# Moving a convolution branch under attention, and a reciprocal root from ScalarE and VectorE to GpSimd, in a conformer layer on eight cores

## The chip, the cores and the metric

The kernel runs on all 8 cores of one Trainium2 chip (two dies, cores 0 to 3 and 4 to 7). Each core computes 2048 of the 2 x 8192 tokens and needs nothing from the others. The metric is the device time of the slowest core, in microseconds (us). Some executions are slow: the cores of one or both dies show a lower granted clock; such runs are left out of every comparison. PE is the tensor engine, ACT is ScalarE, DVE is VectorE, POOL is GpSimd.

## The reference

```python
u = rms_norm(x, norm_mix_pre)
a_val, a_gate, q, k, v = split(u @ w_in)              # 512 + 512 + 3 * 512 columns
h = a_val * sigmoid(a_gate)                           # GLU
h = causal_depthwise_conv(h, dw_w, dw_b)              # 31 taps
conv_out = silu(layer_norm(h, ln_g, ln_b))            # norm over the 512 channels
attn_out = chunked_band_attention(q, k, v, rel_bias)  # 8 heads, chunks of 64, 8 chunks back
mixed = concat([conv_out, attn_out]) @ w_out
h = x + rms_norm(mixed, norm_mix_post)
u = rms_norm(h, norm_ffn_pre)
f = (gelu(gate) * val of causal_depthwise_conv(u @ w_up)) @ w_down
out = h + rms_norm(f, norm_ffn_post)
```

## The kernel before

Every operation is recorded with the buffers that it reads and writes. A list scheduler with a cost model then fixes the order of each engine's instructions when the kernel is built. In the traces each engine takes its queue in that order, and this matters for most of what follows (in wup_early below two DMA issues at the head of POOL's queue stood 3.68 us, and the small operation behind them began 0.08 us after they were done).

The stages, in order, are: input projections; four attention slots, one for each group of 512 tokens (numbered 2 to 5), with other work of PE woven in as fill; the convolution of chunk 0 and of chunk 1 (1024 tokens each); its layer norm, Silu and an exchange through DRAM, which turns the split layout of the convolution into the time layout of the projection; the output projection in 17 tiles of up to 128 tokens; and the FFN. The FFN uses the same banks of PSUM as the projection, so it begins when the projection is nearly done. In the profile's lines `ps` is a tile in PSUM, which PE's matmuls write here, and `big` is one in SBUF, where their operands are (as in `PE L905 MATMUL ps<-big`). Here, in short form, are a chunk's tail and the projection's reciprocal root (rstd):

```python
def conv_norm(ch):                                    # before
    for g in range(0, 32, 4):
        dve.tensor_tensor(v, v, mean, subtract)       # 4 groups of channels x 129, fp32
        dve.tensor_tensor(v, v, rstd, mult)
        for i in range(4):
            act.activation(cs[g + i], cf[g + i], Silu, scale, bias)
    sp.dma_start(out=cd, in_=cs)                      # the exchange: write ...
    sp.dma_start(out=raw, in_=cd)                     # ... and read back in the other layout
    for c in range(4):                                # rearrange (q s) to (s q)
        (act.copy if c == 3 else dve.tensor_copy)(coT[c], raw[c])
...
def wo_sq(i, src):                                    # two for each tile of the projection
    act.activation(junk, src, Square, accum_out=ssq)
    act.activation(tmp, ssq, Sqrt, scale=1.0 / D, bias=eps)
    dve.reciprocal(rstd, tmp)
...
for t in range(17 + 5):                               # the projection, a software pipeline
    for lag, f in ((5, wo_tp), (4, wo_u), (3, wo_sq2), (2, wo_res), (1, wo_sq1), (0, wo_mm)):
        if 0 <= t - lag < 17:
            f(t - lag)
```

`wo_mm` fills one of three pairs of PSUM banks. `wo_sq1` squares it, `wo_res` scales it (DVE) and adds x (DVE). `wo_sq2` squares the sum, `wo_u` scales that (DVE), and `wo_tp` transposes it for the FFN (PE, then an ACT copy).

The softmax here doesn't subtract the row's maximum and nothing guards it: scores larger than these inputs give would overflow.

Of the kernel before, what the change touches and what calls it, by code (L numbers as in the profile page):

```python
# [9 lines left out]
BF16 = mybir.dt.bfloat16  # L10
# [8 lines left out]
AHEAD = {2: 0, 3: 0, 4: 0, 5: 600}  # L19
# [293 lines left out]
def build_program():  # L313
# [11 lines left out]
    cvp_d = dr("cvp", [128, 3 * 32])  # L325
# [11 lines left out]
    CP = {0: 130, 1: 128}  # L337
    cd = {c: nc.dram_tensor("cd%d" % c, [8, 128, 4 * CP[c]], BF16).ap() for c in CN}

    with ExitStack() as es:  # L340
# [38 lines left out]
        blkf = const("blkf", [128])  # L379
# [3 lines left out]
        cvp = const("cvp", [3, 32])  # L383
# [3 lines left out]
        epsc = const("epsc", [1])  # L387
# [30 lines left out]
        cwt = sb("cwt", 151504, [32, 5, 128], BF16)  # L418

        g2b = sb("g2b", gfp.lo, [1024])  # L420
        cfb = [sb("cf0", 102352, [32, 129]), sb("cf1", 12800, [32, 128])]
        st4 = [sb("lnst%d" % i, 118864 + i * 516, [129]) for i in range(4)]
        cs = [sb("cs0", 120960, [32, 130], BF16), sb("cs1", 29184, [32, 128], BF16)]
        cbq = sb("cbq", 200912, [32, 129], BF16)
        raw = [sb("raw0", 120960, [8, 4, 130], BF16), sb("raw1", 120960, [8, 4, 128], BF16)]
        coT = [sb("coT0", 102352, [4, 1032], BF16), sb("coT1", 102352 + 8256, [4, 1024], BF16)]
        Wo = sb("Wo", 135120, [8, 1024], BF16)
# [48 lines left out]
        S.op("pool", lambda: pool.memset(epsc.ap, EPS), writes=[epsc])  # L476
# [301 lines left out]
        def weave(steps, fill):  # L778
            total = sum(c for c, _ in fill)
            done, k = 0.0, 0  # L780
            for i, s_ in enumerate(steps):
                s_()
                while k < len(fill) and done + fill[k][0] / 2 <= total * (i + 1) / len(steps):
                    fill[k][1]()
                    done += fill[k][0]
                    k += 1
            while k < len(fill):
                fill[k][1]()
                k += 1

        c_lo = {0: 0, 1: 129}

        def conv_units(ch):
            N, cf = CN[ch], cfb[ch]
            units = []
            g = 0
            while g < 32:
                ng = min(3, 32 - g)

                def f(g=g, ng=ng):  # L800
                    b = nbank()
                    for i in range(ng):
                        for d in range(5):
                            o_ = c_lo[ch] + 4 - d
                            S.mm(lambda i=i, d=d, o_=o_: pe.matmul(  # L805
                                b.ap[:, i * N:(i + 1) * N], lhsT=cwt.ap[:, g + i, d, :], rhs=hP.ap[:, g + i, o_:o_ + N],
                                start=(i == 0 and d == 0), stop=(i == ng - 1 and d == 4), skip_group_check=True),
                                reads=[cwt[(g + i) // 8], hP[0], hP[1]] + [hP[q] for q in ((2, 3) if ch == 0 else (3, 4, 5))],
                                writes=[b], last=(i == ng - 1 and d == 4), n=145)
                    v = lambda: b.ap[:, :ng * N].rearrange("p (g s) -> p g s", g=ng)  # L810
                    S.op("dve", lambda: dve.scalar_tensor_tensor(
                        out=cf.ap[:, g:g + ng, :N], in0=v(), scalar=0.5,
                        in1=cvp.ap[:, 0, g:g + ng].unsqueeze(2).to_broadcast([128, ng, N]), op0=ALU.mult, op1=ALU.add),
                        reads=[b, cvp], writes=[cf[g + i] for i in range(ng)], n=ng * N)
                    S.bias += 400 * ch
                    S.op("act", lambda: act.activation(out=cbq.ap[:, g:g + ng, :N], in_=cf.ap[:, g:g + ng, :N], func=AF.Square),
                         reads=[cf[g + i] for i in range(ng)], writes=[cbq[g + i] for i in range(ng)], n=ng * N)
                    S.bias -= 400 * ch
                units.append((0.08 * 5 * ng, f))
                g += ng  # L820
            return units

        def conv_stats(ch):
            N, cf = CN[ch], cfb[ch]
            mean, var, t2, rs = st4
            b = nbank()
            for g in range(32):
                S.mm(lambda g=g: pe.matmul(b.ap[:, 0:N], lhsT=blkf.ap, rhs=cf.ap[:, g, :N], start=(g == 0), stop=False, skip_group_check=True),
                     reads=[blkf, cf[g]], writes=[b], last=(g % 8 == 7), n=4 * N)
            for g in range(32):  # L830
                S.mm(lambda g=g: pe.matmul(b.ap[:, N:2 * N], lhsT=blk.ap, rhs=cbq.ap[:, g, :N], start=False, stop=(g == 31), skip_group_check=True),
                     reads=[blk, cbq[g]], writes=[b], last=(g == 31), n=N)
            S.op("dve", lambda: dve.tensor_scalar(out=mean.ap[:, :N], in0=b.ap[:, 0:N], scalar1=1.0 / 512, scalar2=None, op0=ALU.mult),
                 reads=[b], writes=[mean], n=N)
            S.op("dve", lambda: dve.tensor_tensor(out=t2.ap[:, :N], in0=mean.ap[:, :N], in1=mean.ap[:, :N], op=ALU.mult),
                 reads=[mean], writes=[t2], n=N)
            S.op("dve", lambda: dve.scalar_tensor_tensor(out=var.ap[:, :N], in0=b.ap[:, N:2 * N], scalar=1.0 / 512, in1=t2.ap[:, :N],
                                                         op0=ALU.mult, op1=ALU.subtract),
                 reads=[b, t2], writes=[var], n=N)
            S.op("dve", lambda: dve.tensor_scalar(out=var.ap[:, :N], in0=var.ap[:, :N], scalar1=0.0, scalar2=EPS, op0=ALU.max, op1=ALU.add),  # L840
                 reads=[var], writes=[var], n=N)
            S.op("dve", lambda: dve.reciprocal(out=t2.ap[:, :N], in_=var.ap[:, :N]), reads=[var], writes=[t2], n=N, f=8.0)
            S.op("act", lambda: act.activation(out=rs.ap[:, :N], in_=t2.ap[:, :N], func=AF.Sqrt), reads=[t2, DH["exps"]], writes=[rs], n=N + 3000)

        def conv_norm(ch):
            N, cf = CN[ch], cfb[ch]
            mean, var, t2, rs = st4
            for g in range(0, 32, 4):
                keys = [cf[g + i] for i in range(4)]
                v = cf.ap[:, g:g + 4, :N]  # L850
                S.op("dve", lambda: dve.tensor_tensor(out=v, in0=v, in1=mean.ap[:, :N].unsqueeze(1).to_broadcast([128, 4, N]), op=ALU.subtract),
                     reads=keys + [mean], writes=keys, n=4 * N)
                S.op("dve", lambda: dve.tensor_tensor(out=v, in0=v, in1=rs.ap[:, :N].unsqueeze(1).to_broadcast([128, 4, N]), op=ALU.mult),
                     reads=keys + [rs], writes=keys, n=4 * N)
                for i in range(4):
                    S.op("act", lambda i=i: act.activation(out=cs[ch].ap[:, g + i, :N], in_=cf.ap[:, g + i, :N], func=AF.Silu,  # L856
                                                           scale=cvp.ap[:, 1, g + i:g + i + 1], bias=cvp.ap[:, 2, g + i:g + i + 1]),
                         reads=[cf[g + i], cvp], writes=[cs[ch][g + i]], n=N)
            S.dma("sp", "cw%d" % ch, lambda: sp.dma_start(
                out=cd[ch].rearrange("q (c a) z -> (q c) (a z)", c=16), in_=cs[ch].ap.rearrange("p g s -> p (g s)")),  # L860
                reads=[cs[ch][g] for g in range(32)], writes=[DH["cd%d" % ch]], kb=1024)
            S.dma("sp", "cr%d" % ch, lambda: sp.dma_start(
                out=raw[ch].ap.rearrange("p q c s -> p q (c s)"), in_=cd[ch].rearrange("q p z -> p q z")),
                reads=[DH["cd%d" % ch]], writes=[raw[ch]], kb=1024)
            for c in range(4):
                o_ = coT[ch].ap[:, c, :].rearrange("p (s q) -> p s q", q=8)
                i_ = raw[ch].ap[:, :, c, :CN[ch]].rearrange("p q s -> p s q")
                if c == 3:
                    S.op("act", lambda o_=o_, i_=i_: act.copy(out=o_, in_=i_), reads=[raw[ch]], writes=[coT[ch][c]], n=2200)
                else:  # L870
                    S.op("dve", lambda o_=o_, i_=i_: dve.tensor_copy(out=o_, in_=i_), reads=[raw[ch]], writes=[coT[ch][c]], n=1030)
# [271 lines left out]
        def slot(g):  # L1143
            if g == 2:
                pre = pa_units(1) + pa_units(2)
            else:
                pre = pa_units(g)
# [121 lines left out]
```

## Time and profile before

| what | us |
|---|---|
| time, median of 4 runs (range) | 891.35 (890.35 to 892.97) |
| first matmul of the output projection | 332.92 |
| first matmul of the FFN | 414.61 |
| between the two, which I call the projection stage | 81.69 |

The profile is that of the slowest core. Line numbers such as L905 are those of a kernel's own file, so they differ from kernel to kernel. Its page, windows, waits and groups are shown in the prediction below. PE is full in attention and in the FFN, and has holes from 300 to 364 us, so that is where a change can gain.

### The profile page before, as it was taken

The page shows a single profiled execution, that of the slowest core. Times are in us where ns is not written, and L with a number is a line of the kernel's source. Part 1 is how long each engine was busy: PE and PEld are TensorE (multiplying, and loading weights), DVE is VectorE, ACT ScalarE, POOL GpSimd, SP SyncE. Part 2 cuts the span into 40 slices and gives each one's busy share as a digit, 9 for nine tenths or more (in the row PEclk, how much of TensorE's full clock was granted, in tenths as well). Part 3 has the DMA queues.
Part 4 walks back from the last instruction along what each step waited for, and adds up shares of the span by engine and source line. Part 5 has one row for each costly group of instructions (what it writes and reads, how often), then busy time and mean ns, then how long its engine had stood idle before and what let it go on. Part 6 is the DMA issues. An engine that isn't in the chain of part 4 may idle for free.

```text
span 890.2 us, 16644 instructions; the slowest of 8 cores (879.1 to 890.2 us)
## 1 busy us (share of the span) xinstructions
PE 820.8 (92%) x5788; PEld 467.0 (52%) x5788; DVE 561.0 (63%) x750; ACT 508.1 (57%) x721; POOL 129.4 (15%) x213
## 2 busy tenths in 40 slices
PE   2899899999999909698999999999999999999996
PEld 1445344444448804344666666644456666665442
DVE  2676345545455774798888888832358888885232
ACT  4567446545464785697877777711147777773111
POOL 2221000000011001000333333200022222200000
PEclk9999899999999969898999999999999999999999
DMA  8996120303959229775999999723288877810323
GB/s 271 291 305 173 48 25 25 49 1 63 165 61 164 74 96 173 247 249 189 137 132 112 113 112 116 84 71 118 95 154 79 78 72 75 81 13 27 116 94 119
DMA packets 145510, 103.84 MB, mean 117 GB/s; under 512 B 116882, under 2 KB 124434, under 8 KB 144660
## 3 DMA queue, kind: packets, MB, share of 16 engines
q0 software_dynamic: 96704, 36.25, 37.5%
q1 hardware_dynamic: 48148, 65.93, 24.9%
q8 instruction: 48, 0.79, 0.4%
q10 hardware_dynamic: 576, 0.60, 0.2%
q14 instruction: 34, 0.28, 0.1%
HBM read 117.98 MB, written 21.02 MB: 156 GB/s over the span
## 4 chain that ended last, share of the span: by engine, by line
PE 81%; ACT 6%; DMA 5%; DVE 3%; issue 3%; SPq 1%; POOL 0%; ACTq 0%; DVEq 0%; POOLq 0%
PE ps L1021 34%; PE ps L989 17%; PE ps L617 6%; PE ps L567 4%; PE ps L592 4%; PE ps L603 3%; PE ps L733 3%; PE ps L701 3%; ACT big L856 2%; PE ps L905 2%; DMA big<-xw 2%; PE ps L805 2%; ACT big L912 1%; DMA big<-cd 1%; DMA cd<-big 1%
## 5 line engine op out<-in xcount | busy, mean ns | idle before, releaser
L1021 PE MATMUL ps<-big 128*128 128x344 bf16 (+1 forms) x2112 | 314.0, 310 | 1.2 <-DVE big L918 0.4
L1021 PEld LDWEIGHTS ps<-big 128*128 128x128 bf16 x2112 | 205.8, 98 | 108.5 <-issue 1.9
L989 PE MATMUL ps<-big 128*128 128x512 bf16 x704 | 152.3, 379 | 0.0
L1026 ACT COPY big<-ps 128x1032 f32<-128x1032 f32 x88 | 89.7, 1020 | 83.5 <-DVE big L1030 58.5
L1030 DVE SCALAR_TENSOR_TENSOR big<-big 128x1026 f32<-128x1026 f32 x88 | 113.0, 1284 | 32.0 <-ACT big L1027 27.9
L975 POOL DMA_DIRECT2D big<-w_up x88 | 77.3, 881 | 334.4 <-PE ps L1021 185.6
L711 ACT ACTIVATE big<-ps 128x256 bf16<-128x256 f32 (+3 forms) x128 | 90.1, 704 | 52.7 <-PE ps L733 36.1
L1033 DVE SCALAR_TENSOR_TENSOR big<-big 128x1026 f32<-128x1026 f32 x88 | 113.4, 1288 | 10.2 <-DVE big L1030 0.9
L989 PEld LDWEIGHTS ps<-big 128*128 128x128 bf16 x704 | 68.9, 98 | 82.8
L1027 ACT ACTIVATE big<-ps,big 128x1026 f32<-128x1026 f32 x88 | 106.9, 1215 | 0.0
L905 PE MATMUL ps<-big 128*128 128x512 bf16 (+1 forms) x272 | 65.4, 399 | 28.1 <-ACT big L856 20.9
L997 ACT ACTIVATE big<-ps 128x1024 bf16<-128x1024 f32 x16 | 16.4, 1024 | 129.8 <-PE ps L989 129.8
L1001 DVE SCALAR_TENSOR_TENSOR big<-ps,big 128x1024 f32<-128x1024 f32 x16 | 20.5, 1284 | 105.8 <-POOL big L503 105.8
L617 PE MATMUL ps<-big 128*128 128x512 bf16 (+1 forms) x320 | 65.4, 346 | 0.3 <-DVE big L673 0.3
L905 PEld LDWEIGHTS ps<-big 128*128 128x128 bf16 (+1 forms) x272 | 26.5, 101 | 62.1 <-issue 35.6
L1044 DVE TENSOR_TENSOR big<-big 128x1026 bf16<-128x1026 bf16 x44 | 53.8, 1222 | 0.7 <-PE ps L1021 0.4
L716 DVE TENSOR_TENSOR big<-big 128x512 bf16<-128x512 bf16 (+1 forms) x80 | 29.6, 370 | 38.3 <-ACT big L711 37.7
L567 PE MATMUL ps<-big 128*128 128x512 bf16 x168 | 42.5, 403 | 6.3 <-ACT big L495 5.2
L1041 ACT ACTIVATE big<-big 128x1026 bf16<-128x1026 f32 x44 | 46.5, 1058 | 0.4 <-DVE big L1033 0.4
L500 POOL TENSOR_SCALAR big<-big 128x1 f32<-128x1 f32 x37 | 8.0, 217 | 264.9 <-ACT big L997 174.6
L592 PE MATMUL ps<-big 128*128 128x512 bf16 (+1 forms) x192 | 39.3, 352 | 1.0 <-DVE big L595 0.5
L733 PE MATMUL ps<-big 128*128 128x65 bf16 x640 | 39.1, 196 | 0.5 <-issue 0.5
(97 smaller groups left out, 802.2 us busy)
## 6 DMA issues: line engine op xcount, KB each, us to landing
big<-w_up POOLq DMA_DIRECT2D x88, 256.0 KB, 5.7
big<-xw SPq DMA_DIRECT2D x37, 512.0 KB, 5.8
big<-w_in SPq DMA_DIRECT2D x40, 256.0 KB, 8.2
h1s<-big SPq DMA_DIRECT2D x16, 512.0 KB, 3.5
big<-h1s SPq DMA_DIRECT2D x16, 512.0 KB, 4.0
out<-big SPq DMA_DIRECT2D x16, 512.0 KB, 2.9
big<-w_down POOLq DMA_DIRECT2D x22, 256.0 KB, 6.8
big<-cwt POOLq DMA_DIRECT2D x4, 1280.0 KB, 25.5
```

Source lines behind the costliest of these rows:

```text
L567: S.mm(lambda k=k: pe.matmul(b.ap, lhsT=ut.ap[:, k, j * 128:(j + 1) * 128], rhs=Wv.ap[:, k, :], start=(k == 0), stop=(k == 7)), reads=[ut[ ...
L592: S.mm(lambda k=k: pe.matmul(b.ap[:, :N], lhsT=Wk.ap[:, k, c * 128:(c + 1) * 128], rhs=ut.ap[:, k, :N], start=(k == 0), stop=(k == 7)), re ...
L617: S.mm(lambda k=k: pe.matmul(b.ap[:, :n], lhsT=Wa.ap[:, k, col:col + 128], rhs=ut.ap[:, k, n0:N], start=(k == 0), stop=(k == 7)), reads=ut ...
L711: S.op("act", lambda: act.activation(out=p_.ap[:, :, :Nq], in_=s_.ap[:, :, :Nq], func=AF.Exp), reads=[s_], writes=[p_, DH["exps"]], n=2 * Nq)
L905: S.mm(lambda k=k, half=half, l_=l_: pe.matmul(pp.ap[0:n, half, :], lhsT=l_, rhs=Wo.ap[:, k, half * 512:(half + 1) * 512], start=(k == 0), ...
L975: S.dma("pool", "wup%d" % (si % 8), lambda: pool.dma_start(out=wring[si % 8].ap, in_=w_up_v[:, :, cbk * 128:(cbk + 1) * 128]), reads=[coT[ ...
L989: S.mm(lambda f=f, half=half, i=i, pdv=pdv: pe.matmul(pdv[:, half * 512:(half + 1) * 512], lhsT=actb.ap[:, f, i * 128:(i + 1) * 128], rhs= ...
L1021: S.mm(lambda k=k, t=t, n_=n_: pe.matmul(pu.ap[:, t, 0:n_], lhsT=wb.ap[:, k, :], rhs=u2T.ap[:, k, b0 + 342 * t:b0 + 342 * t + n_], start=( ...
L1026: S.op("act", lambda: act.copy(out=xs.ap, in_=pu.ap[:, :, 0:344]), reads=[pu], writes=[xs], n=1032)
L1027: S.op("act", lambda: act.activation(out=ta.ap, in_=pu.ap[:, :, 2:344], func=AF.Identity, scale=fdw.ap[:, cbk, 2:3], bias=fdw.ap[:, cbk, 3 ...
L1030: S.op("dve", lambda: dve.scalar_tensor_tensor(out=tB.ap, in0=xs.ap[:, :, 1:343], scalar=fdw.ap[:, cbk, 1:2], in1=ta.ap, op0=ALU.mult, op1 ...
L1033: S.op("dve", lambda: dve.scalar_tensor_tensor(out=ta.ap, in0=xs.ap[:, :, 0:342], scalar=fdw.ap[:, cbk, 0:1], in1=tB.ap, op0=ALU.mult, op1 ...
```

## The change

The intent is to fill the holes. Chunk 0's whole branch (convolution, norm, exchange, activation) moves into attention slots 4 and 5. Chunk 1 gets cheaper sums, a root without ACT, Silu after the exchange in 4 instructions instead of 32, and an exchange in two halves. The projection's reciprocal root goes to POOL, and the loads of W_out and of the first W_up blocks are issued later. The core of the diff, with cuts:

```diff
-AHEAD = {2: 0, 3: 0, 4: 0, 5: 600}
+AHEAD = {2: 0, 3: 0, 4: 0, 5: 0}
...
+            elif g == 4:
+                fill = [(0, lambda: v_ones(5))] + kvq_units(5) + conv_units(0) + mix(pa_units(4), norm_units(0), 1)
             else:
-                fill += pre
-                fill += conv_units(0)
-                fill += [(3.5, lambda: conv_stats(0))]
+                fill = pa_units(5) + [(0, load_wo)] + conv_units(1) + norm_units(1)
...
+            if ch == 0:      # silu_unit: after the exchange, on the time layout
+                S.op("act", lambda: act.activation(out=t_.ap, in_=r, func=AF.Tanh, scale=..., bias=...), ...)
+                S.op("dve", lambda: dve.tensor_scalar(out=r, in0=r, scalar1=..., scalar2=..., op0=ALU.mult, op1=ALU.add), ...)
+                S.op("dve", lambda: dve.scalar_tensor_tensor(out=o_, in0=sw(t_.ap), scalar=1.0, in1=sw(r), op0=ALU.add, op1=ALU.mult), ...)
+            else:
+                S.op("act", lambda: act.activation(out=o_, in_=sw(r), func=AF.Silu, scale=..., bias=...), ...)
...
             S.op("act", lambda: act.activation(out=junk4.ap[0:n], in_=src, func=AF.Square, accum_out=stat.ap[0:n, c:c + 1]), ...)
-            S.op("act", lambda: act.activation(out=stat..tmp, in_=stat..c, func=AF.Sqrt, scale=1.0 / D, bias=epsc.ap[0:n]), ...)
-            S.op("dve", lambda: dve.reciprocal(out=stat..out, in_=stat..tmp), ...)
+            return rstd_from(c, D, n)     # POOL: tensor_scalar (mult, add), then tensor_tensor (pow -0.5)
...
-                  reads=[coT[0][2]] if si < 6 else [],
+                  reads=[u2T[si + 5]] if si < 6 else [],      # load_wup: W_up's first six blocks
...
+            if 10 <= t < 16: load_wup(t - 10)                 # issued by POOL, inside the projection
```

## The prediction

> **What bounds the kernel now.** I began with the cores view (879.1 to 890.2 us, clock 0.973 to 0.982: no disturbed die), then the page's busy line and its slices.
>
> ```profile
> PE 820.8 (92%) x5788; PEld 467.0 (52%) x5788; DVE 561.0 (63%) x750; ACT 508.1 (57%) x721; POOL 129.4 (15%) x213
> ...
> PE   2899899999999909698999999999999999999996
> ...
> PEclk9999899999999969898999999999999999999999
> ```
>
> A slice is 22.3 us. PE is full almost everywhere: attention up to 265 us, FFN from 414.6 us. The holes are slices 14 to 18. The windows view (engines in us of busy, then granted clock, DMA share, GB/s) shows them:
>
> ```profile
> 211.00:265.00 54.00, 53.25 (x441) 24.79 (x440) 25.76 (x64) 29.65 (x45) 2.92 (x6) 1.00 0.78 118
> 265.00:300.00 35.00, 32.81 (x483) 29.31 (x480) 21.48 (x52) 17.41 (x33) 5.29 (x9) 1.00 0.82 107
> 300.00:335.00 35.00, 13.84 (x141) 11.90 (x142) 25.40 (x39) 32.40 (x74) 2.22 (x3) 0.75 0.30 107
> 335.00:363.00 28.00, 22.06 (x108) 9.59 (x106) 14.25 (x20) 14.63 (x28) 3.03 (x4) 0.93 1.15 223
> 363.00:412.00 49.00, 46.08 (x264) 22.80 (x264) 44.69 (x58) 40.76 (x80) 0.00 (x0) 0.95 0.68 227
> ```
>
> So attention is bound by PE, with DVE and ACT half idle. From 300 to 335 the bound is ACT (32.4 of 35): the 64 Silu instructions of 0.485 us. The waits view of 262 to 434 us and the chain of waits say what PE stood for:
>
> ```profile
> PE ps L905 <- ACT big L856: 20.9, 1, 20.9
> DVE big L871 <- DMA big<-cd: 9.2, 2, 6.0
> PE ps L905 <- DVE big L918: 7.0, 1, 7.0
> ```
> ```profile
> 335.29 10.97 DMA cd<-big
> 346.38 12.74 DMA big<-cd
> 359.21 3.29 DVE big L871 x3
> ```
>
> The output projection (L905) waited 20.9 us for chunk 0's norm and Silu, and then stood again from 356.9 to 364.0 us for chunk 1's, whose exchange through DRAM took 11.0 + 12.7 us. After 386 us the projection runs at 4.12 us a tile: the chain goes through ACT Square, ACT Sqrt, DVE reciprocal, DVE multiply and add, and back. The FFN starts at 414.6 us because it reuses the projection's PSUM banks. From 433 us it is a regular pattern that the diff doesn't touch.
>
> [...]
>
> **The change part by part.**
>
> (1) *fp32 sums become bf16.* The by-form groups of 262 to 412 us:
>
> ```profile
> L828 PE MATMUL ps<-big 128*128 128x129 f32 x64 | 8.1, 278 | 0.0
> L831 PE MATMUL ps<-big 128*128 128x129 bf16 x32 | 2.1, 221 | 0.0
> ```
> Chunk 0's sums cost PE 8.1 + 2.1 = 10.2 us and become 64 bf16 matmuls, 2 x 2.05 = 4.1. Chunk 1 likewise goes from 9.4 to 4.1. About 11 us less, of which chunk 0's 6 lie on the full PE. The price is 22 casts of 387 elements, 16 on POOL and 5 or 6 on ACT, beside other work.
>
> (2) *Chunk 0 moves under attention.* Its convolution (10.5 us of PE), sums, norm (16 DVE instructions of 0.69 = 11 us), exchange and Tanh-Silu (4 Tanh on ACT, about 1.1 us each; 8 DVE instructions, an estimate of 1 to 1.5 us each from L1030's 1.28) go into the 4th and 5th attention slots. In 211 to 300 us DVE was busy 47 of 89, so some 25 us more fit.
>
> (3) *64 Silu on the channel-split layout become 4 on the time layout.* Chunk 1 had 32 x 0.484 = 15.5 us of ACT before its exchange; now 4 instructions of about 2.3 us (the copy at L869, same shape and stride, took 2.34) come after it and take the copies' place. The exchange is cut in halves, so the first half travels while the second is normed.
>
> (4) *The end of attention plus chunk 1, called S.* In the kernel before, group 5's GLU projection begins at 244.8 us with nearly all of attention 5 ahead: a slot is 53 us, of which 40 are fill, so 12.6, less 1.4 done. Now chunk 0's 10.2 + 4.1 come before that point: it begins at 244.8 - 1.4 + 14.3 = 257.7. What follows is 15.2 (GLU) + 14.3 (chunk 1) + 12.6 (attention) = 42 us of dense PE, S = 300. But chunk 1 needs group 5's hidden states through DRAM; with quiet queues the write took 3.3 us (159.6 to 162.9), and the read's median is 9.4. During those 12 us PE has only attention, about half full: 6 us lost. W_out is now loaded after that arrival, 10.8 us to landing plus the issues, which ends near S too. So S = 300 + 6 + 1 = 307.
>
> (5) *The projection from S on.* PE needs 3.90 us a tile (spacing from 370 to 386 us), 17 tiles = 66. The Sqrt and reciprocals of L915 and L918 (0.29 and 0.15 us, two per tile) go to POOL, so the 4.12 us loop opens. DVE per tile:
>
> ```profile
> L931 DVE SCALAR_TENSOR_TENSOR big<-ps,big 128x1024 f32<-128x1024 f32 x14 | 17.9, 1281 | 1.9 <-DVE big L918 1.6 <-PE ps L905 0.2
> L935 DVE TENSOR_TENSOR big<-big 128x1024 f32<-128x1024 f32 x14 | 17.1, 1224 | 1.4
> L948 DVE SCALAR_TENSOR_TENSOR big<-big 128x1024 bf16<-128x1024 f32 x13 | 16.6, 1276 | 0.0
> ```
> That is 1.28 + 1.22 + 1.28 = 3.8. On the same DVE stands chunk 1's tail: 13 dependent small operations at 0.4 us spacing (5 us, in place of the 0.94 us reciprocal and the Sqrt) and 16 x 0.65 = 10.5. So DVE owes 15.5 + 17 x 3.8 = 80 us after S, more than PE's 66: DVE becomes the bound of this stage. The FFN's first matmuls can go when the last but one tile has left PSUM, 5 to 6 us before DVE is done (in the kernel before: 414.6 against 421.2 us). FFN start = 307 + 80 - 5 = 382. Gain: 414.6 - 382 = 32.6 us. The ramp of the first FFN blocks (to 433 us) and all after it I keep. 891.35 - 32 = 859.
>
> **The rivals.**
> - *PE stays the bound.* If chunk 1's norm slips under the end of attention, or the 12 us of waiting are filled, S is 300 and the stage 66 + 3: FFN at 369, time about 846. For it: DVE and ACT are half idle in attention. Against it: the norm can't begin before chunk 1's last sums, the last PE work of the slot.
> - *The exchange of chunk 1 stays exposed.* Norm done at S + 16, then a write and a read of half a MB (7 to 12 us each if they collide with W_out and x as the old ones did), Silu 4.6: S + 35 to S + 45. Tile 9 would start near S + 43 by DVE's pace, so it is hidden or costs up to 5 us, and half of the gain only if the exchange were twice the old one: 864, at worst near 875.
> - *The fuller attention slots stall PE.* DVE would be some 80% busy in the second half of slot 4, and each engine takes its queue in order; an attention mask multiply behind a 1.3 us norm step holds PE. At 0.3 us for each of 37 steps, in two slots, it costs 15 to 20 us: 875 to 880. For it: L716 already waits 20.5 us for ACT. Against it: two score buffers and PE fill of 40 us per slot.
> - *POOL's latency.* Each rstd goes ACT, POOL, POOL, DVE: some 1.3 us against 0.8. The tile lags should hide it; only the last tiles show 1 to 2 us.
>
> **Range and chances.** The middle is 859. Rival one pulls to 846, the exchange and the stalls to 872, and these are the ends. 2% faster is 873.5 us: it takes 18 of the 32 us to be missed. Faster 0.89, within 2% 0.09, slower 0.02.
>
> **What would show each step.** Right: PE full until about 300 us; convolution matmuls of chunk 0 before group 5's GLU; no Sqrt and no f32 matmul; the first FFN matmul at 378 to 386 us; DVE over 90% busy from S on, with chunk 1's norm first and the projection waiting for PSUM; the two halves' exchange ended before tile 9. A PE hole of some 6 us before chunk 1's convolution, released by the hidden states' DMA. Wrong: a first FFN matmul before 372 us (DVE not the bound), a stand of the projection on the exchange or on W_out of over 5 us, or attention slots of clearly more than their PE work; a changed FFN from 20 us after its start on would refute that the rest stays.

The sum: S = 307, FFN start 307 + 80 - 5 = 382, gain 414.6 - 382 = 32.6, and 891.35 - 32 = 859. The trace of the kernel before shows this: five table loads of 1.28 us each on ACT between 295 and 341 us; 0.687 us for each of the norm's DVE instructions of 516 elements (L851, L853), the 0.69 of part (2); and after PE's stand of 6.97 us 5.74 us for the projection's next 16 matmuls, 3.62 in the tile after it. The 1.1 us for a Tanh in part (2) is an estimate, near the 1.06 us of ACT's L1041 on 1026 elements in that trace. That chunk 0's Tanh runs among attention's exps without a table load, on which part (2) relies, was not shown then; the trace after shows it (below).

## The result, and the profile after

The changed kernel took **877.81 us** (median of 10 runs; fast runs from 875.63, two slow ones of 960.62 and 1002.87) against 892.33 for the kernel before in the same rounds. The ratio is **0.984**, 95% interval 0.9825 to 0.9855: 14.5 us faster by the medians, but within 2%, and outside the predicted range of 846 to 872. The median is that of all ten runs; of the eight fast ones it is 877.6. A ratio here is always the mean time of one kernel's fast runs over that of the other's of the same rounds, so it is not quite the ratio of the medians.

The profile is of core 5, span 874.3 us (cores 867.7 to 874.3, clocks 0.976 to 0.984: undisturbed). The page's busy line and slices of 21.9 us:

```profile
PE 813.6 (93%) x5724; PEld 460.2 (53%) x5724; DVE 561.2 (64%) x738; ACT 481.6 (55%) x628; POOL 185.5 (21%) x296
...
PE   2899999999997788898999999999999999999996
...
PEclk9997999999998898999999999999999999999998
```

The deep hole is gone; a shallow one, of 7s and 8s from slice 13 to 19, is left. The first matmuls of the projection (L978) and of the FFN (L1088), from the timeline (start, duration, engine, line; in brackets the idle time and what ended it):

```profile
311.79 10.63 PE L978 MATMUL ps<-big 128*2 128x512 bf16 x48 [0.49 <-issue]
```
```profile
397.44 1.83 PE L1088 MATMUL ps<-big 128*128 128x344 bf16 x7 [0.48 <-DVE big L998]
```

So the projection starts 332.92 - 311.79 = 21.1 us earlier, but the FFN only 414.61 - 397.44 = 17.2 us: the projection stage **grew** from 81.69 to 85.65 us. The windows view (us, busy PE, PEld, DVE, ACT, POOL, then clock, DMA share, GB/s):

```profile
275.80:289.00 13.20, 5.84 (x56) 3.27 (x56) 10.10 (x18) 10.13 (x14) 0.00 (x0) 0.60 0.82 120
...
309.00:325.00 16.00, 12.13 (x68) 5.29 (x65) 14.64 (x34) 2.22 (x4) 7.98 (x5) 1.00 0.80 176
325.00:345.00 20.00, 17.10 (x88) 7.70 (x88) 12.54 (x13) 14.49 (x20) 6.69 (x13) 0.91 0.86 254
345.00:365.00 20.00, 17.36 (x92) 8.25 (x93) 14.59 (x12) 17.23 (x23) 8.41 (x17) 0.91 0.56 164
365.00:400.00 35.00, 27.93 (x171) 14.31 (x169) 29.53 (x24) 24.90 (x40) 28.02 (x38) 0.97 1.12 253
```

DVE is full only in the first 16 us of the stage. From 325 to 365 no engine looks full on average, though PE (17.36 of 20, at a clock of 0.91) and ACT (17.23) come near it at the end, and from 365 on POOL is busy 28.02 of 35 us where it was nearly idle before. The waits view (255 to 425 us; us in total, times, longest):

```profile
POOL big L505 <- ACT big L985: 34.5, 12, 7.5
...
DVE big L998 <- POOL big L508: 10.1, 11, 2.6
...
PE ps L978 <- DVE big L998: 9.1, 10, 3.0
```

This is a chain: PE's matmul waits for DVE's eviction (L998), which waits for POOL's root (L505, then L508), which waits for ACT's Square (L985). Before, `PE ps L905` waited 20.9 us for the Silu and 7.0 for DVE; now PE waits 9.1 us in ten pieces for a loop that runs through POOL. One turn of the loop, first POOL, then DVE:

```profile
374.86 0.18 POOL L505 TENSOR_SCALAR big<-big 128x1 f32<-128x1 f32 x1
375.19 0.56 POOL L508 TENSOR_TENSOR big<-big 128x1 f32<-128x1 f32 x1
375.83 1.02 POOL L505 TENSOR_SCALAR big<-big 128x1 f32<-128x1 f32 x1
377.00 1.40 POOL L508 TENSOR_TENSOR big<-big 128x1 f32<-128x1 f32 x1
378.37 0.94 POOL L1042 DMA_DIRECT2D big<-w_up  x1
```
```profile
375.58 1.22 DVE L1002 TENSOR_TENSOR big<-big 128x1024 f32<-128x1024 f32 x1 [0.17 <-DVE big L998]
376.72 1.28 DVE L1015 SCALAR_TENSOR_TENSOR big<-big 128x1024 bf16<-128x1024 f32 x1
378.65 1.28 DVE L998 SCALAR_TENSOR_TENSOR big<-ps,big 128x1024 f32<-128x1024 f32 x1 [0.65 <-POOL big L508]
```

Three things are to be seen. No POOL line has a bracket: POOL goes from one instruction to the next without waiting, and the next turn starts at 379.39, so its own queue takes 4.53 us a tile. That is the distance of the tiles here (374.12 to 378.65 for L998), against 4.12 before. DVE closes the turn: L998 stands 0.65 us for its root, because POOL's last L508 ends at 378.40, 0.4 us after L1015. Second, the same instruction on the same 128 numbers takes 0.18 or 1.02 us (L505), 0.56 or 1.40 (L508). The long ones lie beside L1002 and L1015, the two DVE instructions that read two SBUF operands. Over the eight cores, from 300 to 420 us, the 104 L505 that began beside L998, which reads one operand from PSUM, took 0.18 to 0.19 us, and the 64 that began beside L1002 0.46 to 1.19. (The page calls spans on POOL rough; from start to start the long ones take 1.17 and 1.37 us here, which says the same.) Third, a DMA issue of W_up (256 KB) takes 0.94 us of POOL's queue. The most drastic case is at the head of the stage, where chunk 1's norm reads two SBUF operands without a pause:

```profile
317.16 5.97 POOL L505 TENSOR_SCALAR big<-big 2x1 f32<-2x1 f32 x1 [7.46 <-ACT big L985]
```
```profile
318.19 4.89 DVE L901 TENSOR_TENSOR big<-big 128x512 bf16<-128x512 f32 x8
```

A POOL instruction on two numbers took 5.97 us, and ended with the norm. In the middle of the stage ACT does this:

```profile
335.11 1.28 ACT L931 ACT_TABLE_LOAD   x1
336.40 4.23 ACT L931 ACTIVATE big<-big 128x1024 bf16<-128x1024 bf16 x2
```

A second pair of Silu follows at 344.72 with 4.21 us: 9.7 us of ACT, in blocks in which no tile's Square can run. The tiles of this stretch are about 6 us apart on average (L998 from 332.27 to 356.02, four tiles, singly 3.7 to 9.0).

Ahead of the stage, the wait for group 5's hidden states stands where it was expected. The chain of work that ended last has it as `275.85 5.39 DMA hd<-big` and `281.30 7.82 DMA big<-hd`, after which chunk 1's convolution starts at 289.25. From the FFN on all is as before: its regular pattern begins at 416.43 us, against 433.10.

### The profile page after: what moved, and what is told of

Same layout as the page of the kernel before. It is cut to its first block, busy times and chain, and to the rows that moved or that the text cites. A ratio compares the mean times of both kernels' runs of the same rounds, so it can differ in the third digit from the quotient of the medians.

```text
span 874.3 us, 16588 instructions; the slowest of 8 cores (867.7 to 874.3 us)
## 1 busy us (share of the span) xinstructions
PE 813.6 (93%) x5724; PEld 460.2 (53%) x5724; DVE 561.2 (64%) x738; ACT 481.6 (55%) x628; POOL 185.5 (21%) x296
## 4 chain that ended last, share of the span: by engine, by line
PE 80%; DMA 5%; POOL 4%; issue 4%; ACT 3%; DVE 3%; SPq 1%; ACTq 0%; DVEq 0%; POOLq 0%
PE ps L1088 35%; PE ps L1056 17%; PE ps L622 5%; PE ps L572 4%; PE ps L597 4%; PE ps L608 3%; PE ps L706 3%; PE ps L738 3%; PE ps L814 2%; DMA big<-xw 2%; POOL big L505 2%; POOL big L508 2%; PE ps L978 2%; DMA hd<-big 1%; DMA big<-hd 1%
## 5 line engine op out<-in xcount | busy, mean ns | idle before, releaser
L1088 PE MATMUL ps<-big 128*128 128x344 bf16 (+1 forms) x2112 | 314.2, 310 | 2.5 <-ACT big L1093 1.7
L1088 PEld LDWEIGHTS ps<-big 128*128 128x128 bf16 x2112 | 205.8, 98 | 109.8 <-issue 3.3
L505 POOL TENSOR_SCALAR big<-big 128x1 f32<-128x1 f32 x71 | 29.4, 414 | 292.9 <-ACT big L1064 174.6
L978 PE MATMUL ps<-big 128*128 128x512 bf16 (+1 forms) x272 | 64.4, 394 | 9.6 <-DVE big L998 9.1
L622 PE MATMUL ps<-big 128*128 128x512 bf16 (+1 forms) x320 | 63.1, 340 | 0.3 <-ACT big L626 0.2
L508 POOL TENSOR_TENSOR big<-big 128x1 f32<-128x1 f32 x71 | 47.9, 675 | 10.4
L978 PEld LDWEIGHTS ps<-big 128*128 128x128 bf16 (+1 forms) x272 | 26.2, 100 | 43.3 <-issue 16.4
L706 PE MATMUL ps<-big 64*128 64x128 bf16 (+3 forms) x256 | 39.1, 317 | 7.1 <-ACT big L716 7.0
## 6 DMA issues: line engine op xcount, KB each, us to landing
big<-cwt POOLq DMA_DIRECT2D x2, 1920.0 KB, 15.9
```

The source lines that it names most:

```text
L508: S.op("pool", lambda: pool.tensor_tensor(out=stat.ap[0:n, out:out + 1], in0=stat.ap[0:n, tmp:tmp + 1], in1=nh.ap[0:n], op=ALU.pow), reads ...
L622: S.mm(lambda k=k: pe.matmul(b.ap[:, :n], lhsT=Wa.ap[:, k, col:col + 128], rhs=ut.ap[:, k, n0:N], start=(k == 0), stop=(k == 7)), reads=ut ...
L978: S.mm(lambda k=k, half=half, l_=l_: pe.matmul(pp.ap[0:n, half, :], lhsT=l_, rhs=Wo.ap[:, k, half * 512:(half + 1) * 512], start=(k == 0), ...
L1088: S.mm(lambda k=k, t=t, n_=n_: pe.matmul(pu.ap[:, t, 0:n_], lhsT=wb.ap[:, k, :], rhs=u2T.ap[:, k, b0 + 342 * t:b0 + 342 * t + n_], start=( ...
```

## The experiments

My theory after this reading was that the projection stage's excess comes from the loop through POOL (long roots and W_up issues in one queue) and from Silu's blocks on ACT. The rivals were that DVE's sum of work is a floor, as I had predicted, and that the late start of the stage is the larger loss. Fifteen kernels are told of here, the changed one with them. The diffs are shortened, names and arguments too. "Stage" is from the first projection matmul to the first FFN matmul, on the slowest core of the profile. The time is the median of all runs, slow ones too (two of ten for the changed kernel, one each for rstd_act, b_pool, silu_short, pow1_spread and no_hp5_late_silu); the ratio uses fast runs alone. For no_hp5_late_silu this matters: its fast runs have a median of 874.79.

| kernel | right result | time, us | ratio to before (95%) | first projection mm | first FFN mm | stage |
|---|---|---|---|---|---|---|
| before | yes | 892.33 | 1 | 332.92 | 414.61 | 81.7 |
| changed | yes | 877.81 | 0.9840 (0.9825 to 0.9855) | 311.79 | 397.44 | 85.7 |
| rstd_act | yes | 878.17 | 0.9837 (0.9811 to 0.9863) | 316.11 | 402.59 | 86.5 |
| b_pool | yes | 894.28 | 1.0029 (1.0006 to 1.0052) | 335.31 | 416.90 | 81.6 |
| port | no | 880.01 | one run | 316.10 | 401.92 | 85.8 |
| wup_early | yes | 878.17 | 0.9851 (0.9819 to 0.9882) | 313.88 | 400.27 | 86.4 |
| pow1 | yes | 871.91 | 0.9779 (0.9755 to 0.9802) | 315.49 | 395.02 | 79.5 |
| pow1_wup | yes | 875.78 | 0.9819 (0.9795 to 0.9843) | 314.81 | 396.77 | 82.0 |
| silu_short | no | 870.06 | 0.9762 (0.9737 to 0.9786) | 311.85 | 392.77 | 80.9 |
| pow1_silu_short | no | 864.83 | 0.9684 (0.9663 to 0.9706) | 313.00 | 387.67 | 74.7 |
| pow1_spread | yes | 870.05 | 0.9755 (0.9730 to 0.9781) | 314.43 | 393.00 | 78.6 |
| pow1_tanh | yes | 872.07 | 0.9794 (0.9769 to 0.9819) | 312.84 | 394.33 | 81.5 |
| pow1_spread_w | yes | 889.12 | 0.9955 (0.9930 to 0.9980) | 321.60 | 412.86 | 91.3 |
| no_hp5 | no | 874.00 | 0.9802 (0.9779 to 0.9824) | 311.36 | 398.25 | 86.9 |
| no_hp5_late_silu | no | 876.81 | 0.9831 (0.9798 to 0.9864) | 312.39 | 397.63 | 85.2 |
| no_hp5_no_dve0 | no | 871.63 | 0.9758 (0.9737 to 0.9779) | 309.44 | 394.45 | 85.0 |

Two columns give their own error bars. Ten kernels (the changed one, and the nine others from rstd_act to pow1_tanh without b_pool) have the same order of instructions up to the first projection matmul, and there it lies between 311.79 and 316.11 us, depending on the core that was profiled. The changed kernel and the three no_hp5 have the same work in the stage, and there it lies between 85.0 and 86.9. So a stage of one core is known to 1 to 2 us.

The traces hold all eight cores of the profiled run, which gives a better measure. Means over the eight cores, in us:

| kernel | first projection mm | stage (lowest and highest core) |
|---|---|---|
| before | 329.9 | 80.7 (78.6, 81.7) |
| changed | 309.9 | 85.2 (84.0, 85.7) |
| pow1 | 312.6 | 79.1 (77.8, 79.5) |
| silu_short | 309.6 | 80.9 (80.9, 80.9) |
| pow1_silu_short | 311.7 | 74.0 (73.6, 74.7) |
| no_hp5 | 308.4 | 85.4 (84.0, 86.9) |
| no_hp5_late_silu | 309.9 | 85.0 (83.5, 85.2) |
| no_hp5_no_dve0 | 305.7 | 84.8 (83.8, 87.1) |

### rstd_act: the projection's root back to ACT and DVE

```diff
-            return rstd_from(c, D, n)
+            act.activation(tmp, ssq, Sqrt, scale=1.0 / D, bias=eps)
+            dve.reciprocal(rstd, tmp)
```

> Undo of one part: the projection's rstd as in the kernel before (ACT Sqrt and DVE reciprocal), all else changed. POOL theory: a tile costs 4.1 us as before, but chunk 1's Silu lies in the middle of the projection, so each change between Sqrt and Silu loads a table (1.28 us each, 3 to 5 loads); net 3 to 8 us faster than the changed kernel, 870 to 875. Rival (POOL's rstd is a help, as the change means it): 2 to 6 us slower than the changed kernel, 880 to 884.

Undoing this part changed nothing: 0.9837 against 0.9840. Neither expectation came true. The tiles at the end were then 4.12 us apart again, as before the change (33.0 us from tile 8's eviction to tile 16's, against 35.8). In return the first half was longer (56.2 us from the first matmul to tile 8's eviction, against 53.3), where three table loads for Sqrt and two for Silu alternated on ACT, 1.28 us each. So the root's move to POOL opened no loop: it traded ACT's table loads for POOL's queue.

### b_pool: the kernel before, with only the root on POOL

```diff
-            act.activation(tmp, ssq, Sqrt, scale=1.0 / D, bias=eps)
-            dve.reciprocal(rstd, tmp)
+            return rstd_from(c, D, n)
```

> The kernel before with one part alone of the change: the projection's rstd on POOL. There W_up's loads are issued before the projection, so POOL has only the rstd. POOL theory: POOL's queue holds two stretched pairs a tile, 3.2 us without W_up's issue of 0.94, under the 4.1 us loop; the pace falls to about 3.9 to 4.1 or stays, and the time changes by -3 to +2 us. Rival (any rstd through POOL costs by latency alone): the pace rises to 4.4 or more and the time by 3 to 6 us.

By itself this part of the change makes the old kernel slower by 0.29% (interval 0.06 to 0.52), about 2.5 us, which lies between the two expectations. Its stage is 81.6 us, like before: the first half is shorter (49.6 us to tile 8's eviction, against 51.4) and tile 8 to tile 16 longer (35.1 against 33.0). POOL was busy 17.9 of 30 us from 380 on, without W_up issues in the loop. Up to there tiles 3.80 and 4.52 us apart mostly alternate, but the last four are 4.52 apart, the pace of the changed kernel, although POOL waits in each turn:

```profile
412.48 1.20 POOL L500 TENSOR_SCALAR big<-big 128x1 f32<-128x1 f32 x1 [0.80 <-ACT big L912]
```
```profile
415.47 1.28 DVE L925 SCALAR_TENSOR_TENSOR big<-ps,big 128x1024 f32<-128x1024 f32 x1 [0.65 <-POOL big L503]
```

So a full POOL queue isn't the only way to this pace. What both kernels share is that DVE's eviction stands 0.65 us for a root whose last POOL instruction ends only after DVE's own two-operand instruction.

### port: the residual add reads PSUM in place of an SBUF tile

```diff
-            dve.tensor_tensor(h, h, x, add)          # two SBUF inputs
+            dve.tensor_tensor(h, psum_tile, x, add)  # one from PSUM, one from SBUF
```

> Wrong result on purpose: the residual add on DVE reads the PSUM tile again instead of the SBUF tile just written, so of its two tensors only one is in SBUF. Same length on DVE. Theory[...] (a POOL instruction stands while DVE reads two SBUF tensors): the L505 beside it falls from 1.02 us to 0.19, while the one beside the norm of chunk 1 (5.97 us) stays and so does the L508 beside the scaling by g (two SBUF tensors still). Rival (POOL is slow for reasons of its own[...]): L505 stays at 1.02.

This tests what stretches POOL's instructions. The groups by shape, 365 to 390 us, of the changed kernel and then of this one (count, us in total, mean ns):

```profile
L505 POOL TENSOR_SCALAR big<-big 128x1 f32<-128x1 f32 x12 | 7.2, 600 | 1.0
```
```profile
L505 POOL TENSOR_SCALAR big<-big 128x1 f32<-128x1 f32 x12 | 2.3, 188 | 1.2 <-ACT big L985 0.4
```

With the second SBUF operand gone, every one of them takes its short time, 0.19 us. The add itself kept its length (1.22 us on average in both). L508 still has long ones, as of 1.63 us at 379.21, and that one lies beside the other DVE instruction with two SBUF inputs (L1015, 379.16 to 380.44). The one beside chunk 1's norm stayed at 5.97. Over the eight cores 36 L505 began beside L1002, and all took 0.18 to 0.19 us. So for L505 beside the add the cause of the stretching is shown: DVE's second SBUF operand (0.46 to 1.19 us with it, 0.18 to 0.19 without). But the stage stayed at 85.8, with tiles in a new rhythm of 3.5 and 4.9 to 5.9 us. This can't be read as "the stretching costs nothing": the add now holds its pair of PSUM banks for about 1.4 us longer, and the scheduler changed its order a little for that. What the stretching costs is left to the next experiments.

### wup_early and pow1_wup: W_up's issues out of the projection's last third

```diff
-                  reads=[u2T[si + 5]] if si < 6 else [],
+                  reads=[coT[1][3]] if si < 6 else [],      # chunk 1's last Silu
...
-            if 10 <= t < 16: load_wup(t - 10)
+            if t == 8: all six
```

> The first six W_up loads are gated on chunk 1's last Silu (about 349 us) instead of on tiles 5 to 10 of the projection, so their six issues of 0.94 us leave POOL's queue in the last third. POOL queue theory: the pace of tiles 11 to 16 falls from 4.53 us to about 4.2 (the kernel before with rstd on POOL and no W_up issue showed 4.16 to 4.3), so 2 us off at the end, less what the bunched issues cost near 350 us: time -3 to 0 us against the changed kernel. Rival (the latency of the chain ACT, POOL, POOL, DVE sets the pace, not the queue): pace stays 4.5.

> Both of the above together. POOL theory: nothing is left of POOL's queue, pace 3.9, FFN start 6 to 10 us earlier, time 868 to 872. Rival: as the better of the two alone.

wup_early took 878.17 us, no gain. Tile 8 to tile 16 fell from 35.8 to 33.6 us (4.2 a tile as expected, in turns of 3.80 and 4.52), but the first half rose from 53.3 to 56.2. The timeline of POOL shows why:

```profile
351.63 1.83 POOL L1042 DMA_DIRECT2D big<-w_up  x2 [3.68 <-ACT big L931]
353.54 0.19 POOL L505 TENSOR_SCALAR big<-big 128x1 f32<-128x1 f32 x1
```

The issues waited 3.68 us for the Silu at the head of POOL's queue, and a tile's root waited behind them. A wait that was taken from one place in an in-order queue came back in another. With pow1 (next) the same move made the stage 2.5 us longer, and 875.78 us misses both of its expectations.

### pow1: one POOL instruction for each root instead of two

```diff
-            act.activation(junk, src, Square, accum_out=ssq)
-            pool.tensor_scalar(tmp, ssq, 1.0 / D, EPS, mult, add)
-            pool.tensor_tensor(rstd, tmp, nh, pow)
+            act.activation(junk, src, Square, scale=1.0 / 32, accum_out=msq)   # 1/32 squared is 1/D
+            pool.tensor_tensor(rstd, msq, nh, pow)
```

The epsilon of 1e-6 is left out for tiles of 128 rows; the result passed the comparison with the reference. Where a row could be all zero this is no substitute.

> One POOL instruction for each rstd of the 128-row tiles instead of two: Square is scaled by 1/32, so its sum is the mean, and the scaling step (which also adds the epsilon of 1e-6, here left out; means are near 1) goes. POOL theory: POOL's work a tile falls by the two L505 (0.18 + 1.02 us) and the chain by one step; pace 4.53 to 3.9 to 4.1; FFN start 5 to 8 us earlier; time 870 to 874. Rival (DVE order and Silu set it): under 2 us.

871.91 us, ratio 0.9779, and the intervals of this and of the changed kernel don't touch. The stage fell by 6.1 us to 79.5, most of it at the end: tile 8 to tile 16 took 30.1 us, 3.8 a tile. POOL then works for 3.0 us a tile (0.91 + 0.57 + 1.55) and waits for the rest, while DVE goes on without waiting for it: 3.79 us from eviction to eviction, with 23.38 of 25 us busy from 365 to 390, and PE 24.82. So the roots' way through POOL held up the last third of the changed kernel, at a cost of 6 us, and with it shortened DVE and PE are full there, as the prediction had expected. pow1 shortens POOL's queue and the chain from Square to eviction at once, so it doesn't say which of the two counted; b_pool's last tiles show that the chain alone can do it.

### silu_short: chunk 1's Silu replaced by a short Tanh

```diff
-                act.activation(out=coT in time order, in_=sw(r), func=AF.Silu, ...)
+                act.activation(out=coT in memory order, in_=r, func=AF.Tanh, ...)
```

> Wrong on purpose (outputs are wrong, shapes and work otherwise the same): the changed kernel with chunk 1's four Silu instructions replaced by Tanh read and written in the order of memory, about 1.05 us each in place of 2.1, with no table load in the projection. It measures the Silu's share of the loss by itself. Theory A (the 9.7 us of Silu and table load inside the projection cost about 10 us of its 85.6): with 5.5 us of ScalarE gone, the stretch from the first matmul to tile 8's eviction falls from 53.3 to 48 to 50 us and the time to 873 to 875. Rival (the loss in that stretch comes from chunk 1's norm on VectorE, 11 us at its head, and Silu lies beside it): 53 us stays, 877 to 879.

Each instruction took 1.23 us in place of 2.16 and the table load of 1.28 was gone: 5.0 us less on ACT. The time from the first matmul to tile 8's eviction fell from 53.3 to 48.5, within the expected 48 to 50, and the stage by 4.7 to 80.9. So ACT's time in this stretch goes into the stage nearly one for one. The whole time fell by more than I had expected (0.9840 to 0.9762 is 7.0 us of 892). As a mean over the eight cores of the two profiled runs the first FFN matmul comes 4.6 us earlier (390.5 against 395.1) and the span is 5.1 shorter; the 2 us beyond that differ with the run and the slowest core, and are left open.

### pow1_silu_short: both together

> Wrong on purpose, to see whether the two costs found in the projection add up: one GpSimd instruction per reciprocal root (pow1: 79.5 us from the first projection matmul to the first FFN matmul, in place of 85.7) and chunk 1's Silu replaced by a short Tanh in memory order (silu_short: 80.9). Theory A (the two costs are in different parts of the stage, 6.1 and 4.7 us, and add up): 74 to 76 us, which is what the prediction gave the stage, and a time of 864 to 868. Rival (they overlap, or VectorE at 66 us busy plus the norm's head sets a floor): 77 to 79 us, 869 to 871.

The stage is 74.7 us. The two costs were 6.1 and 4.7, and 85.65 - 6.1 - 4.7 = 74.9: they add up (as means over the eight cores 6.2 and 4.3 of 85.2 leave 74.7, and 74.0 is measured). So the 10.6 us by which the stage missed are accounted for, by the roots' way through POOL and by part of Silu's time on ACT. DVE is no floor above this. That 74.7 is also the 75 us of the prediction is in part luck: the prediction had DVE full through the stage, and here it was busy 66.26 of 74.67 us, and full (21.80 of 22.67, at 3.79 us a tile) only from 365 us on. Chunk 1's tail took it 11.3 us after the first projection matmul, not 15.5.

### pow1_spread and pow1_tanh: two right kernels that try to get Silu's share

```diff
-LATE = ((100, 100), (0, 0))
+LATE = ((100, 100), (0, 300))        # pow1_spread: one Silu after each tile's Square, not pairs
```
```diff
-            if ch == 0:
+            if True:                  # pow1_tanh: chunk 1 in the Tanh form too, DVE does the multiply
```

> Correct kernel: the changed kernel with one GpSimd instruction per reciprocal root (as pow1, 871.91 us) and with chunk 1's four Silu instructions given a lower priority, so that they stand one after each tile's Square instead of two and two back to back. Theory A (Silu blocks ScalarE for 4.2 us at a time, and the projection's three pairs of PSUM banks can't bridge a block): the stretch of the projection in which tiles 4 to 8 go, 52 us from its first matmul to tile 8's eviction in pow1, shortens by 2 to 4 us, and the time falls to 868 to 870. Rival (ScalarE is simply full in this stretch: 22.8 of 25 us busy, so the order of its work doesn't matter): 871 to 873, within 1 us of pow1.

> Correct kernel: pow1 with chunk 1's activation in the Tanh form too, as chunk 0 has it: ScalarE gives 4 Tanh of about 1.1 us in place of 4 Silu of 2.1 us and loses the table load of 1.28 us in the projection[...], VectorE gets 4 times 0.55 + 2.0 us more. Theory A (ScalarE is what the middle of the projection waits for): 5 us less on ScalarE, against 10 us more on VectorE, which was busy 16.3 of 25 us there: net 1 to 3 us faster than pow1, 869 to 871. Rival (VectorE becomes what it waits for): 873 to 877.

pow1_spread took **870.05 us**, ratio 0.9755: the fastest right kernel, and faster than both kernels of the change. Against pow1 its gain is open: the stage is 78.6 against 79.5, the intervals overlap, and they ran in different rounds. The stage fell by about 1 us (as a mean over the eight cores from 79.1 to 78.0) where the shorter Silu had given 4.7, so most of Silu's cost is ACT's time and not the blocks. pow1_tanh gave 872.07 and a stage of 81.5: what ACT gave up, DVE's 10 us took back (DVE busy 74.94 of 81.49 us). It falls between the two expectations, and it isn't better than pow1.

### pow1_spread_w: the rearrangement on the write instead of the read

```diff
-    act.activation(out=o_, in_=sw(r), func=AF.Silu, ...)    # reads with a step, writes in order
+    act.activation(out=ow, in_=r, func=AF.Silu, ...)        # reads in order, writes with a step of 16 bytes
```

> Correct kernel, the candidate for the best: pow1_spread (870.05 us) with the activation's rearrangement from the exchange's order to time order moved from the read to the write: inputs read in the order of memory, output written with a step of 16 bytes. A single Silu on ScalarE took 2.14 to 2.20 us and chunk 0's VectorE multiply 2.02 us with the rearrangement on the read; read and written in the order of memory (silu_short) the ScalarE instruction took about 1.19. Theory A (the reading side's step is what doubles the duration, so a stepped write is free): Silu 1.1 us, the multiply 1.3 us, the projection 4 us shorter than 78.6, time 865 to 868. Rival (a stepped write costs the same): durations stay at 2.1 and 2.0, time 869 to 871.

Both theories missed. Silu's group in the changed kernel and in this one:

```profile
L931 ACT ACTIVATE big<-big 128x1024 bf16<-128x1024 bf16 x4 | 8.4, 2160 | 0.0
```
```profile
L931 ACT ACTIVATE big<-big 128x1024 bf16<-128x1024 bf16 x4 | 19.8, 4957 | 0.0
```

With the stepped write (8 bf16, that is 16 bytes) a Silu took 4.96 us, where with the stepped read (256 elements) it had taken 2.16; a Tanh read and written in order took 1.23 (silu_short). On DVE chunk 0's multiply went from 2.02 us with the stepped read to 4.80 with the stepped write. The stage became 91.3 us, and the stretch before it was longer too, because chunk 0's multiply runs there. (In this round six of the eleven runs of the kernel before were slow, 908.86 us and more; the ratio uses the five from 892.09 to 895.42.)

### no_hp5, no_hp5_late_silu, no_hp5_no_dve0: what holds the start of the stage

```diff
 # no_hp5: chunk 1's convolution reads the columns of earlier groups
-                    o_ = c_lo[ch] + 4 - d
+                    o_ = 4 - d
-                        [hP[q] for q in ((2, 3) if ch == 0 else (3, 4, 5))]
+                        [hP[2], hP[3]]
 # no_hp5_late_silu: and chunk 0's activation gets a lower priority
-LATE = ((100, 100), (0, 0))
+LATE = ((100, 3000), (0, 0))
 # no_hp5_no_dve0: or, chunk 0's activation is one Tanh on ACT, without its 8 DVE instructions
```

> Wrong result on purpose: chunk 1's convolution reads chunk 0's columns, so it doesn't wait for group 5's hidden states through DRAM. Theory that the wait (13.3 us, PE busy 5.8 of them) is paid in full: the end of attention and chunk 1's sums come about 7 us earlier (302 in place of 309), the FFN starts 5 to 7 us earlier, 871 to 873. Rival (W_out's arrival, which hangs on the same hidden states, or the exchange of chunk 1 takes its place): under 2 us.

> Wrong on purpose, as no_hp5 (chunk 1's convolution doesn't wait for group 5's hidden states), and in addition chunk 0's Tanh-form activation on VectorE gets a lower priority, so that its 2.0 us instructions don't stand ahead of the convolution's evictions. no_hp5 alone moved the end of the sums by 0.3 us only (308.86 against 309.2). Theory B (two waits lie side by side: the hidden states, and VectorE's in-order queue with chunk 0's activation): now the end of the sums comes 5 to 9 us earlier, about 300 to 304, the first projection matmul follows, and the time is 866 to 871. Rival (it is the tensor engine's own work, with the clock at 0.60 to 0.9 there, that fills this stretch): the end of the sums moves by under 2 us, 873 to 876.

> Wrong on purpose, to close the question of the stretch ahead of the projection: as no_hp5 (chunk 1's convolution doesn't wait for group 5's hidden states), and chunk 0's activation is a single Tanh on ScalarE that writes its result itself, so that the 4 times 0.55 + 2.0 us on VectorE are gone altogether. In no_hp5 they stood ahead of the convolution's evictions, in no_hp5_late_silu ahead of the last attention group's masks, and the sums ended at 309 to 311 in both; the convolution alone ended 12 us earlier in the second. Theory B (both waits are real, and each hides behind the other): without either, the end of the sums comes at 297 to 302 and the time falls by 8 to 12 us against no_hp5, 863 to 867. Rival (the tail of the last attention slot, with its chain from scores to transposes, ends no earlier than 303 to 304 whatever VectorE does, and the sums stand behind it in the tensor engine's order): sums end at 307 to 310, 872 to 875.

Without the wait on the hidden states the sums ended at 308.86 us on the profiled core, where the changed kernel has 309.2: nothing was won there. In its trace chunk 0's multiplies on DVE (2.0 us each, L928) now stood ahead of the convolution's evictions. Moved behind them, in no_hp5_late_silu, they let the convolution end at 291.3 us, 12 us earlier than 303. But then they stood ahead of the last attention masks, and the sums, which follow the attention's tail in PE's queue, began only at 304.56. With neither, the convolution ended at about 292, the attention's tail at about 300, and the sums followed, to 306.1 us on the profiled core, 3 us earlier than in the changed kernel.

The slowest core misleads here. As means over the eight cores the sums end at 307.3 us in the changed kernel, at 305.8 in no_hp5, at 308.2 in no_hp5_late_silu and at 301.8 in no_hp5_no_dve0. So no_hp5 does win 1.5 us there, which is part of the 0.4% by which its ratio is better, and the two removals together win 5.5: my expectation of 297 to 302 holds for the mean, and the rival's 307 to 310 doesn't. The whole time, 0.9758 against 0.9840, is 7 us less, but 871.63 is above my 863 to 867. One reason is what comes next, on all eight cores:

```profile
309.44 5.88 PE L981 MATMUL ps<-big 128*2 128x512 bf16 x26 [1.22 <-DMA big<-w_out]
```

The projection now waits 0.5 to 3.0 us for W_out, whose load is still tied to the hidden states. The scheduler orders each of these three kernels a little differently, so they aren't pure removals. But they agree that several things lie side by side before the stage: the hidden states' way through DRAM, chunk 0's 10 us on DVE, the tail of the last attention slot, and close behind them W_out. To remove one is worth 0 to 1.5 us; the first two together are worth 4.2 at the first projection matmul (305.7 against 309.9).

## Why the prediction was wrong

The direction was right and its chance of "faster by over 2%" was far too high: 32 us were promised and 14.5 came.

- **The reading of what bounds the kernel** held. The 20.9 us stand for the Silu and the 7 us stand for the exchange are gone, and attention took the added work without stalling PE (from 211 to 275.8 us PE was busy 63.87 of 64.80). Up to there the rival of stalled attention slots is refuted; in attention's tail chunk 0's activation did stand in DVE's queue, as the no_hp5 kernels show. The exchange of chunk 1 wasn't exposed. One reading was wrong, though. The "4.12 us loop" of the kernel before is no loop through ACT: from 386 to 412 us its DVE was busy 24.34 of 26 us and stood for nothing but its own reciprocal, 0.17 us each time. The 4.12 us were DVE's queue, its three long instructions and two reciprocals, so what the move could win was 4.12 - 3.79 = 0.33 us a tile.
- **Steps (1) to (3)** held in kind: chunk 1's sums took PE 3.9 us (4.1 expected), a Silu 2.16 (2.3), chunk 0's eight DVE instructions 10.2 (8 to 12), and chunk 0's Tanh ran among attention's exps without a table load (the three loads of ACT's trace begin at 6.40, 335.11 and 413.02 us). The expected hole ahead of chunk 1's convolution was there and released by the hidden states.
- **Step (4), S = 307,** came out at 311.8 on the profiled core, and at 307.5 to 311.8 on the eight cores (mean 309.9): 3 to 5 us late. The wait was sized at 6 us of lost PE time. In the 13.2 us from 275.8 PE did 5.84 us of work at a mean clock of 0.60, which is about 3.5 us at full clock (my estimate from these two), so it cost nearly 10. The experiments showed that the wait isn't alone there: with it gone the sums ended 1.5 us earlier as a mean over the cores, with chunk 0's DVE work gone too 5.5.
- **Step (5) is the step that failed**: "The Sqrt and reciprocals of L915 and L918 go to POOL, so the 4.12 us loop opens", and "DVE becomes the bound of this stage". The stage took 85.65 us instead of 75. The pace went up, not down: the roots went through POOL, whose turn takes 4.53 us a tile, because the second root of each tile takes 1.02 + 1.40 = 2.42 us beside DVE's two-operand reads, where the first takes 0.18 + 0.56 = 0.74, and the W_up issues stand in the same queue. This was worth 6.1 us (pow1). The rival "POOL's latency" named the right chain, but took it to cost 1 to 2 us at the end, where it cost 0.4 us in every tile: it counted the short durations (1.3 us against 0.8), not those beside DVE's two-operand reads. That DVE is the bound came true only where the roots were shortened (pow1, 3.79 us a tile).
- **The same step left ACT out of the sum.** Step (3) counted the four Silu as taking the copies' place. They stand in the middle of the projection, where ACT has 3.3 us of Squares and copies for each tile of about 4 us, and so nearly no room for 9.7 us more. Half of that was measured at 4.7 us (silu_short). Together the two terms give the missing 10.6 us (pow1_silu_short: 74.7 us), though the 75 itself was met in part by luck, as said there.
- **DVE over 90% busy from S on** held for 16 us (14.64 of 16.00), and then it was 63% (12.54 of 20.00).
- **Slips in its sums.** 421.2 - 414.6 is 6.6 us, not "5 to 6". To fall short of 2% takes a miss of 14 of the 32 us, not 18 (2% is 17.9 us of gain), so the margin behind the 0.89 was smaller than it said. And 0.3 us (my assumption, which no trace gives) for 37 steps in two slots is 22 us, not 15 to 20.
- **The FFN from its regular part on** is unchanged, as predicted: it begins 16.7 us earlier, and the span is 15.9 us shorter.

## What to carry to other kernels

Moving a small dependent operation to an idle engine was not free here, where that engine took it in order with other things (4.53 us a tile on POOL, against 4.12 before): add up that engine's whole queue for one turn of the loop, at the durations it has beside the other engines' work (here 1.02 us for L505, not 0.18), and compare this with the pace you want. Do such a sum for every engine in every part of a stage, since an average (ACT busy 56.29 of the stage's 85.65 us) can hide a stretch that is nearly full (17.23 of 20 from 345 us on). Where one wait is taken away, look first at which chains end just behind it, and look on all cores: the slowest one can be the exception.
